# A hybrid decoder layer: the delta rule's triangular inverse and block merges for two heads at once, with a new order of issue

## The chip, the cores and the metric

One core of one Trainium2 chip. The metric is device microseconds of one execution, as the median of several runs.

## The reference

One layer works on 1024 tokens of width 1024 in 32-bit floats. After an RMS norm, one projection gives the columns of two groups of heads. Group A is a gated delta rule with 4 heads of width 128, group B a sparse attention with an indexer: each token scores all earlier tokens, keeps the best 256, and attends to them with 8 heads of width 64. Both outputs go through one output projection and a gated addition. What matters here is group A, in chunks of 64 tokens:

```
kkt = jnp.einsum('bhncd,bhnsd->bhncs', k_beta, k) * decay
a_mat = eye + jnp.where(strict, kkt, 0.0)
t_mat = lax.linalg.triangular_solve(a_mat, jnp.broadcast_to(eye, a_mat.shape),
                                    left_side=True, lower=True, unit_diagonal=True)
value = jnp.einsum('bhncs,bhnse->bhnce', t_mat, v_beta)
...
def step(state, inp):
    qd, kd, val, kcd, att, gl = inp
    v_new = val - jnp.einsum('bhcd,bhde->bhce', kcd, state)
    o = jnp.einsum('bhcd,bhde->bhce', qd, state) + jnp.einsum('bhcs,bhse->bhce', att, v_new)
    state = state * gl[..., None, None] + jnp.einsum('bhcd,bhce->bhde', kd, v_new)
    return state, o
```

`t_mat`, the inverse of a unit lower triangular matrix, is what the change computes in another grouping. The kernel uses chunks of 128 tokens, so 8 matrices of 128x128 per head; the result is the same.

## The kernel before, in words

The program is first recorded as a list of operations with what each depends on (`Plan`), and then issued in the order of a table of numbers, `TURNS` (line 76 and on): each number says which of the operations still left comes next. All engines' instructions are issued that way, in `issue`, so the trace shows line 556 for every one of them (554 after the change), and each engine's order is what the table says. Instructions are told apart by their tiles. PSUM tiles of one pool share a name in the trace: `s` for the small products of group A, `mm` for projections, `rec` for the recurrence's products, `po` for its outputs, `g` for the tail.

Stages in time: input norm, transposes and the gates' parameters; then the indexer's scores, to about 200 us; then a long middle of projections (`mm`, three matmuls for one full-precision product, from a high and a low half of both operands), beside which run group A's heads and the indexer's search for the 256th score; from about 560 us on the attention, the output projection and, as a tail, the gate.

In the middle, VectorE (`junk`) and ScalarE (`junka`) count how many scores lie above a threshold, pass after pass, until the threshold is found; after that VectorE makes a mask (`eq`, `cum`) and ScalarE copies it over the scores (`score<-eq`).

Each head h of group A goes through these steps:
- `gdn_s1` (line 1387): norms of q and k, decay matrices, the negated strict lower part `NB` of the 8 matrices (two tiles of four), the product `att`, the transposed and scaled values `v` (by ScalarE).
- `inverse` (line 1576), beside it: `NB` goes to DRAM and comes back as 16x16 diagonal blocks, one per partition group (`Bb`). Fifteen rounds of a product and a sum on VectorE (`ftmp<-Ub,Bb`, `Ub<-ftmp`) invert all blocks of the head. The result goes through DRAM to the tile `U32`, which holds 32x32 diagonal blocks.
- `merge` (line 1607) puts blocks of 16 together to 32, then 64, then 128. Each step is two products with a copy between: `w0` (64 instructions of 32x32x16, `s<-T,NB`), its copy `W0` by ScalarE (`W<-s` of 128x128), `x2` (`s<-U,W`), an addition and a transpose by VectorE (`U32`, `T32`); then `wa` (`s<-T,NB` of 32x32), two copies `W` by ScalarE (`W<-s` of 32x256), `wb` (`s<-W,U` and `s<-U,W`), copies into `T64` by VectorE and into `U` by ScalarE; then `wc` (64x64), its copy into `T64` by ScalarE (`T<-s` of 64x512), and `wd`, whose copy completes `U`.
- `gdn_s2` (line 1487): the recurrence over 8 chunks, a chain of three products (`rec`) a chunk with a VectorE step behind each (`r`, `vnew`, `S`).
- `gdn_out` (line 1551): the norm of the outputs and their way to DRAM.

In `merge` and `gdn_s2` the table puts projection matmuls between the products, so that TensorE has work while a copy is made. Before the change the four heads merge one after the other, at 262, 330, 408 and 486 us, and each head's recurrence runs in part beside the next head's merge.

In the tail, VectorE makes `m0Bl`, `h1Al` and `t1l` (low halves of operands of the last products), GpSimd makes other such halves (`low`, `sl`), and TensorE waits for them in the order of the table.

## Time and profile before

| what | value |
|---|---|
| median of 3 runs | 833.31 us (832.12 to 833.95) |
| the profiled execution, its own time | 835.29 us |
| its span in the trace | 833.3 us |
| mean granted clock of TensorE | 0.984 |
| busy share of PE, DVE, ACT, POOL | 97%, 80%, 71%, 65% |
| chain that ended last | PE 80%, DVE 9%, ACT 6%, issue 2% |
| half clock from, for | 75.62 us, 6.83; 410.13, 10.24; 741.22, 6.83; 829.96 to the end |
| waits of PE above 1.4 us in total | for `t1l` 3.4, for `g` 2.2, for `W` 2.2, for `ident` 1.5 |

The profiled execution took 835.29 us, 2.0 more than its span, and 2.0 more than the median of the runs. A trace row gives start, duration, engine, line, operation, output and inputs, shape, and in brackets the idle time before it and what ended that. Matmuls overlap with the one before them: one of 512 columns is shown with 0.39 to 0.40 us, but in a dense stretch the next starts 0.23 us later. The clock is recorded in windows of 3.41 us.

### The profile page before, as it was taken

To read this page: it belongs to the slowest core of one execution; us is meant where nothing else is said; L and a number is where in the kernel's file an instruction comes from. 1 tells how busy PE (TensorE), PEld (TensorE's weight loads), DVE (VectorE), ACT (ScalarE), POOL (GpSimd) and SP (SyncE) were. 2 spreads that over 40 slices of the span, in tenths; PEclk is the share of its full clock that TensorE was granted. 3 is DMA by queue.
4 is the path that set the end of the run, shared out by engine and by line. 5 is a ranking of instruction groups with operands and counts; after the bars stand their busy time and mean duration, and the time that the engine had idled before them with its cause. 6 is when DMAs were issued, how large, how long until landed. Compare 5 with 4: busy or idle time off the path is not lost.

```text
span 833.3 us, 14829 instructions
## 1 busy us (share of the span) xinstructions
PE 811.9 (97%) x5063; PEld 692.2 (83%) x5063; DVE 664.9 (80%) x1475; ACT 589.6 (71%) x1345; POOL 540.9 (65%) x704
## 2 busy tenths in 40 slices
PE   9998999999999999999999999999999999979996
PEld 6996999987888888888888888878888888768885
DVE  3698757888999999998768854699998786586676
ACT  5765466667999989999775543499886678765342
POOL 3487667524876677577748545368675647988982
PEclk9998999999999999999899999999999999989999
DMA  8963421001122233113312332676313421522453
GB/s 276 371 241 103 159 85 64 1 13 52 39 70 62 89 84 106 58 52 96 87 52 76 87 91 70 219 218 209 113 51 103 155 71 53 197 94 64 140 172 130
DMA packets 77868, 93.14 MB, mean 112 GB/s; under 512 B 24000, under 2 KB 40672, under 8 KB 77664
## 3 DMA queue, kind: packets, MB, share of 16 engines
q1 hardware_dynamic: 77792, 92.20, 34.4%
q8 instruction: 39, 0.64, 0.3%
q14 instruction: 37, 0.30, 0.1%
HBM read 66.72 MB, written 25.45 MB: 111 GB/s over the span
## 4 chain that ended last, share of the span: by engine, by line
PE 80%; DVE 9%; ACT 6%; issue 2%; DMA 1%; POOL 1%; SPq 0%; DVEq 0%; ACTq 0%
PE mm L556 44%; PE g L556 8%; PE lg L556 6%; PE s L556 5%; PE pv L556 4%; PE S L556 4%; PE pt L556 3%; PE c L556 3%; PE rec L556 2%; ACT junka L556 2%; PE po L556 2%; DVE c L556 1%; DVE xT L556 1%; DVE score L556 1%; DVE g L556 1%
## 5 line engine op out<-in xcount | busy, mean ns | idle before, releaser
L556 PE MATMUL mm<-hThi,hiw 128*128 128x512 f32 x400 | 156.8, 405 | 0.6 <-ACT fst L556 0.3
L556 PE MATMUL mm<-hTlo,hiw 128*128 128x512 f32 x400 | 156.3, 402 | 0.0
L556 PE MATMUL mm<-hThi,low 128*128 128x512 f32 x400 | 155.4, 401 | 0.0
L556 POOL TENSOR_TENSOR low<-raww,hiw 128x512 fp32r<-128x512 f32 (+1 forms) x93 | 123.7, 1335 | 43.0 <-ACT hiw L556 26.4
L556 ACT ACTIVATE junka<-score,nt 128x768 bf16<-128x768 int16 (+5 forms) x96 | 99.7, 1039 | 2.5 <-POOL scr L556 0.4
L556 PEld LDWEIGHTS mm<-hThi,hiw 128*128 128x128 f32 x400 | 75.8, 191 | 14.9 <-ACT fst L556 0.7
L556 PEld LDWEIGHTS mm<-hThi,low 128*128 128x128 f32 x400 | 75.9, 190 | 13.9
L556 PEld LDWEIGHTS mm<-hTlo,hiw 128*128 128x128 f32 x400 | 75.8, 190 | 13.6
L556 POOL TENSOR_SCALAR P<-P,rsum 128x128 f32<-128x128 f32 (+7 forms) x64 | 49.1, 773 | 38.0 <-DVE rsum L556 37.4
L556 DVE TENSOR_SCALAR_CACHE_REDUCE junk<-score,cand 128x384 bf16<-128x384 f32 (+2 forms) x96 | 71.1, 740 | 1.3
L556 ACT ACTIVATE hiw<-raww 128x512 fp32r<-128x512 f32 x91 | 56.7, 627 | 19.8 <-PE g L556 8.5
L556 POOL TENSOR_SCALAR nt<-acca,upa 128x1 f32<-128x1 f32 x96 | 36.8, 385 | 40.7 <-ACT junka L556 36.7
L556 ACT ACTIVATE relu<-lg 128x384 f32<-128x384 f32 (+1 forms) x80 | 41.1, 523 | 28.3 <-PE lg L556 24.6
L556 DVE SCALAR_TENSOR_TENSOR score<-relu,sm,score 128x384 f32<-128x384 f32 (+5 forms) x42 | 48.9, 1177 | 11.1 <-ACT relu L556 10.9
L556 ACT ACTIVATE P<-P,mn 128x128 f32<-128x128 f32 (+7 forms) x64 | 49.4, 773 | 11.8 <-DVE mn L556 11.4
L556 DVE TENSOR_TENSOR pl<-pt,ph 128x512 fp32r<-128x512 f32 x72 | 48.3, 685 | 8.2 <-ACT ph L556 6.7
L556 PE MATMUL S<-kst,qT 128*128 128x384 f32 (+2 forms) x192 | 52.3, 354 | 0.3 <-DVE mn L556 0.2
L556 ACT ACTIVATE ph<-pt 128x512 fp32r<-128x512 f32 x72 | 40.9, 594 | 10.4 <-PE pt L556 8.1
L556 ACT ACTIVATE fst<-mm 128x512 f32<-128x512 f32 (+2 forms) x61 | 29.9, 502 | 17.6 <-PE mm L556 17.3
L556 PE MATMUL pt<-ident,P 128*128 128x128 f32 x288 | 40.8, 274 | 0.3 <-POOL P L556 0.2
L556 PEld LDWEIGHTS S<-kst,qT 128*128 128x128 f32 x192 | 34.2, 189 | 7.0 <-DVE mn L556 1.5
L556 DVE SCALAR_TENSOR_TENSOR acc<-fst,cw,acc 128x512 f32<-128x512 f32 x48 | 38.7, 819 | 1.1 <-ACT fst L556 0.4
(434 smaller groups left out, 2507.3 us busy)
## 6 DMA issues: line engine op xcount, KB each, us to landing
raww<-in_w_ct_dram SPq DMA_DIRECT2D x50, 256.0 KB, 2.7
raww<-in_w_out_dram SPq DMA_DIRECT2D x32, 256.0 KB, 3.9
xt<-in_x_dram SPq DMA_DIRECT2D x8, 512.0 KB, 6.4
xc<-in_xc_dram SPq DMA_DIRECT2D x8, 512.0 KB, 7.1
pled<-plt SPq DMA_DIRECT2D x16, 256.0 KB, 4.7
rawi<-in_w_ct_dram SPq DMA_DIRECT2D x16, 256.0 KB, 2.9
pld<-pled SPq DMA_DIRECT2D x16, 256.0 KB, 2.6
out_dram<-gth SPq DMA_DIRECT2D x15, 256.0 KB
```

The costliest lines, as they stand in the source:

```text
L556: r = getattr(getattr(self.nc, o.eng), fn)(*[real(x) for x in args], **{k: real(v) for k, v in kw.items()})
```

## The change

Heads 0 and 1, and heads 2 and 3, now go through `inverse` and `merge` together. `inverse(hs)` has blocks of both heads in one `Bb` and one `Ub`, so that there are 30 products and 30 sums of twice the length instead of 60 and 60; the DMAs stay as many. `merge` takes `w0`, `x2`, `wa` and `wb` of both heads as one group into one PSUM tile, with one copy (W0: 128x256 instead of 128x128; W: two of 32x512 instead of two of 32x256) behind it; `wc` and `wd` stay one group per head. `U32`, `T32`, `W`, `W0` and `T64` are twice as long, and `NB` has four buffers instead of two. The new `gdn_group` runs `gdn_s1` of both heads up to the values, and then one merge for both. So the recurrence of a group's first head starts only behind the second head's preparation.

The table `TURNS` is new as a whole. Up to the end of the indexer's scores the instructions stand nearly where they stood; behind them the order is another one, in the tail also, where the computation is the same.

```diff
+GROUPS = ((0, 1), (2, 3))
...
-c-rlH2Yg(|dFRZ$UiR(2?Y%c(8-N8Ci{6RCf)1h*od5{1q7ftk0tDE=PKu<&B8t605~)H-BrRD<B-u(NpJhw&xy5oj=aNf)@z1t$J}16=U}Rg>Maf+fAOF9_+u5C&Z@&57
...
+c-rlH2XtK3x$fR)pWe^RIWuQ^AN5h08A+p2@4Z*ck|j6UisdFtw&mV!T)=<}#<&t}u)#E&M-LDPfi&9VLIQz=+z?2)cRh0RSSxw!9YM;?dT*t#b@LwnG^2ga(SP>-_y7O<
...
-            nb = NB[n] = half("NB", 2)
+            nb = NB[n] = half("NB", 4)
...
-        yield f"u{h}", UY
-        U = self.Uf[h % 2]
-        yield from self.merge(h, NB, self.U.pop(h), U)
-        self.s1[h] = dict(q=q, U=U, vt=vt, kh=kh, k=k, att=att, ssq=ssq, br=br)
+        self.pre[h] = dict(NB=NB, q=q, U=self.Uf[h % 2], vt=vt, kh=kh, k=k, att=att, ssq=ssq, br=br)
+
+    def gdn_group(self, hs):
+        for h in hs:
+            yield from self.gdn_s1(h)
+        yield f"u{hs[0]}", UY
+        d = [self.pre.pop(h) for h in hs]
+        yield from self.merge([x.pop("NB") for x in d], self.U.pop(hs[0]), [x["U"] for x in d])
+        self.s1.update(zip(hs, d))
...
-    def inverse(self, h):
-        nc, p = self.nc, self.gp
-        yield f"nb{h}"
-        NB = self.NB.pop(h)
+    def inverse(self, hs):
+        nc, p, n = self.nc, self.gp, len(hs)
+        for h in hs:
+            yield f"nb{h}"
         CH = 128 * 129
-        dN = self.tc.dram_tile([8 * CH], F32, name=f"dN{h}")
-        dU = self.dU[h % 2]
         mat = lambda d, n: d.raw(4 * n * CH, ap=[[128, 128], [CH, 4], [1, 128]])
         blk = lambda d, o, r: d.raw(o, ap=[[16 * 129, 64], [128, r], [1, 16]])
-        for n in range(2):
-            nc.sync.dma_start(mat(dN, n), NB[n])
-        Bb = p.tile([128, 16, 16], F32, name="Bb", bufs=1)
-        for g in range(2):
-            nc.sync.dma_start(Bb[64 * g:64 * g + 64], blk(dN, 0, 16))
-        nc.vector.memset(Bb.rearrange("p i l -> p (i l)")[:, 0:256:17], 1.0)
-        Ub = p.tile([128, 8, 16], F32, name="Ub", bufs=1)
-        tmp = p.tile([128, 8, 16], F32, name="ftmp", bufs=1)
-        nc.vector.tensor_copy(Ub, self.eyeb)
+        Bb = p.tile([128, 2, 16, 16], F32, name="Bb", bufs=1)[:, :n]
+        for i, h in enumerate(hs):
+            NB = self.NB.pop(h)
+            dN = self.tc.dram_tile([8 * CH], F32, name=f"dN{h}")
+            for e in range(2):
+                nc.sync.dma_start(mat(dN, e), NB[e])
+            for g in range(2):
+                nc.sync.dma_start(Bb[64 * g:64 * g + 64, i], blk(dN, 0, 16))
+        nc.vector.memset(Bb.rearrange("p h i l -> p h (i l)")[:, :, 0:256:17], 1.0)
+        Ub = p.tile([128, 2, 8, 16], F32, name="Ub", bufs=1)[:, :n]
+        tmp = p.tile([128, 2, 8, 16], F32, name="ftmp", bufs=1)[:, :n]
+        nc.vector.tensor_copy(Ub, self.eyeb[:, None].to_broadcast([128, n, 8, 16]))
         yield BY
         for l in range(1, 16):
-            nc.vector.tensor_tensor(tmp[:, :, :l + 1], Ub[:, :, :l + 1],
-                                    Bb[:, None, :l + 1, l].to_broadcast([128, 8, l + 1]), op=OP.mult)
-            nc.vector.tensor_reduce(Ub[:, :, l:l + 1], tmp[:, :, :l + 1], axis=AX.X, op=OP.add)
+            nc.vector.tensor_tensor(tmp[:, :, :, :l + 1], Ub[:, :, :, :l + 1],
+                                    Bb[:, :, None, :l + 1, l].to_broadcast([128, n, 8, l + 1]), op=OP.mult)
+            nc.vector.tensor_reduce(Ub[:, :, :, l:l + 1], tmp[:, :, :, :l + 1], axis=AX.X, op=OP.add)
             yield 1
-        for g in range(2):
-            nc.sync.dma_start(blk(dU, g * 8 * 128, 8), Ub[64 * g:64 * g + 64])
-        u = self.U[h] = p.tile([128, 8, 32], F32, name="U32", bufs=1)
-        for a in range(4):
-            nc.sync.dma_start(u[32 * a:32 * a + 32], dU.raw(a * 32 * 129, ap=[[128, 32], [CH, 8], [1, 32]]))
-        self.mark(f"u{h}")
-
...
+    def merge(self, NB, u, U):
+        nc, p, m = self.nc, self.gp, len(NB)
+        n = 8 * m
+        full = lambda nm: p.tile([128, 8 * 2, 32], F32, name=nm, bufs=1)[:, :n]
+        u = u[:, :n]
         quad = [slice(32 * a, 32 * a + 32) for a in range(4)]
         b32 = [(32 * a, 32 * a + 32, 32 * a + 64) for a in (0, 2)]
         flat = lambda t: t.rearrange("p a b -> p (a b)")
+        ps = lambda nm, w, n=n: self.ps_s(nm).rearrange("p a b -> p (a b)")[:, :n * w].rearrange("p (a b) -> p a b", b=w)
+        nb = lambda c, r, k: NB[c // 8][c // 4 % 2][r, c % 4, k]
+        T = full("T32")
         nc.vector.transpose(flat(T), flat(u))
         yield F1
         w0 = ps("w0", 16)
+        for c in range(n):
             for q in quad:
                 nc.tensor.matmul(w0[q, c], nb(c, q, q), T[q, c, 0:16], start=True, stop=True)
+        nc.scalar.activation(self.W0[:, :n, 0:16], w0, AF.Copy)
         yield F2
         x2 = ps("x2", 16)
+        for c in range(n):
             for q in quad:
                 nc.tensor.matmul(x2[q, c], self.W0[q, c], u[q, c, 16:32], start=True, stop=True)
         nc.vector.tensor_tensor(u[:, :, 16:32], u[:, :, 16:32], x2, op=OP.add)
+        T = full("T32")
         nc.vector.transpose(flat(T), flat(u))
         for a in (0, 1):
+            nc.gpsimd.tensor_copy(self.T64[quad[a], :n, 32 * a:32 * a + 32], T[quad[a]])
         yield F2
+        W = full("W")
         wa = ps("wa", 32)
+        for c in range(n):
             for i0, i1, i2 in b32:
                 nc.tensor.matmul(wa[i1:i2, c], nb(c, slice(i0, i1), slice(i1, i2)), T[i0:i1, c], start=True, stop=True)
         for i0, i1, i2 in b32:
             nc.scalar.activation(W[i1:i2], wa[i1:i2], AF.Copy)
+        for i in range(m):
+            for q in quad[::-1]:
+                nc.gpsimd.tensor_copy(U[i][q, :, q], u[q, 8 * i:8 * i + 8])
         yield F2
         wb = ps("wb", 32)
+        for c in range(n):
             nc.tensor.matmul(wb[32:64, c], u[32:64, c], W[32:64, c], start=True, stop=True)
             for i0, i1, i2 in b32:
                 nc.tensor.matmul(wb[i0:i1, c], W[i1:i2, c], u[i1:i2, c], start=True, stop=True)
+        nc.vector.tensor_copy(self.T64[32:64, :n, 0:32], wb[32:64])
+        for i in range(m):
+            for i0, i1, i2 in b32:
+                nc.scalar.activation(U[i][i0:i1, :, i1:i2], wb[i0:i1, 8 * i:8 * i + 8], AF.Copy)
         yield F2
         W2 = self.T64
+        wc = []
+        for i in range(m):
+            wc.append(ps("wc", 64, 8))
+            for c in range(8):
+                nc.tensor.matmul(wc[i][64:128, c], nb(8 * i + c, slice(0, 64), slice(64, 128)), self.T64[0:64, 8 * i + c],
+                                 start=True, stop=True)
+        for i in range(m):
+            nc.scalar.activation(W2[64:128, 8 * i:8 * i + 8], wc[i][64:128], AF.Copy)
         yield F2
+        wd = []
+        for i in range(m):
+            wd.append(ps("wd", 64, 8))
+            for c in range(8):
+                nc.tensor.matmul(wd[i][0:64, c], W2[64:128, 8 * i + c], U[i][64:128, c, 64:128], start=True, stop=True)
+        for i in range(m):
+            nc.scalar.activation(U[i][0:64, :, 64:128], wd[i][0:64], AF.Copy)
...
-            self.W0 = p.tile([128, 8, 32], F32, name="W0")
+            self.W0 = p.tile([128, 16, 32], F32, name="W0")
...
-            self.T64 = p.tile([128, 8, 64], F32, name="T64")
+            self.T64 = p.tile([128, 16, 64], F32, name="T64")
...
-            s1 = Chain(x for h in range(4) for x in self.gdn_s1(h))
-            si = Chain(x for h in range(4) for x in self.inverse(h))
+            s1 = Chain(x for hs in GROUPS for x in self.gdn_group(hs))
+            si = Chain(x for hs in GROUPS for x in self.inverse(hs))
```

Instructions: TensorE 4331 as before, VectorE 1306 (1378), ScalarE 1074 (1080), GpSimd 705 (709), SyncE 380 as before.

**TensorE, from wa to wb of the first merge.** Before, behind `wa` (the two rows of `s<-T,NB`) of the first head:

```order
L556 MATMUL s_2030<-T_0_1942,NB_1935 32x32 x8
L556 MATMUL s_2030<-T_0_1942,NB_1937 32x32 x8
L556 MATMUL mm_77<-hThi_124,hiw_107 128x512
L556 MATMUL mm_77<-hTlo_125,hiw_107 128x512
L556 MATMUL mm_75<-hTlo_125,hiw_113 128x512
L556 MATMUL mm_75<-hThi_124,low_114 128x512
L556 MATMUL mm_77<-hThi_124,low_108 128x512
L556 MATMUL s_2031<-W_1943,U_0_1941 32x32
L556 MATMUL s_2031<-U_0_1941,W_1943 32x32 x2
```

After, from the filler behind `x2` of the first group:

```order
L554 MATMUL mm_76<-hThi_124,hiw_111 128x512
L554 MATMUL mm_75<-hTlo_125,hiw_111 128x512
L554 MATMUL mm_75<-hThi_124,low_112 128x512
L554 MATMUL mm_75<-hThi_124,hiw_113 128x512
L554 MATMUL mm_76<-hTlo_125,hiw_111 128x512
L554 MATMUL mm_76<-hThi_124,low_112 128x512
L554 MATMUL s_2038<-T_0_1939,NB_1930 32x32 x8
L554 MATMUL s_2038<-T_0_1939,NB_1932 32x32 x8
L554 MATMUL s_2038<-T_0_1939,NB_1934 32x32 x8
L554 MATMUL s_2038<-T_0_1939,NB_1935 32x32 x8
L554 MATMUL s_2039<-W_1940,U_0_1938 32x32
L554 MATMUL s_2039<-U_0_1938,W_1940 32x32 x2
```

Five projection matmuls stood between `wa` and `wb`; now `wb` follows `wa` directly, and six stand between `x2` and `wa`.

**ScalarE, from W to the copy of wc in the first merge.** Before, in the first head (`T_0<-s` of 64x512 is the copy of `wc`, which `wd` reads):

```order
L556 ACTIVATE W_1943<-s_2030 32x256 x2
L556 ACTIVATE junka_1975,acca_1976<-score_120,nt_0_1977 128x768
L556 ACTIVATE hiw_109<-raww_116 128x512
L556 ACTIVATE scr_1934<-scr_1930,gg_98 128x128 x2
L556 ACTIVATE U_1948<-s_2031 32x8x32 x2
L556 ACTIVATE scr_1933<-scr_1929,gg_98 128x128
L556 ACTIVATE fst_129<-accq_1990 128x512
L556 ACTIVATE scr_1933<-scr_1929,gg_98 128x128
L556 ACTIVATE T_0_1928<-s_2032 64x512
```

After, in the first group, up to the same copy:

```order
L554 ACTIVATE junka_1972,acca_1973<-score_120,nt_0_1966 128x1024
L554 ACTIVATE scr_1929<-scr_1925,gg_98 128x128
L554 ACTIVATE junka_1972,acca_1973<-score_120,nt_0_1974 128x768
L554 ACTIVATE junka_1972,acca_1973<-score_120,nt_0_1974 128x896
L554 ACTIVATE junka_1972,acca_1973<-score_120,nt_0_1974 128x1024
L554 ACTIVATE U_1945<-s_2039 32x8x32
L554 ACTIVATE junka_1972,acca_1973<-score_120,nt_0_1966 128x768
L554 ACTIVATE U_1990<-s_2039 32x8x32
L554 ACTIVATE U_1945<-s_2039 32x8x32
L554 ACTIVATE junka_1972,acca_1973<-score_120,nt_0_1966 128x896
L554 ACTIVATE U_1990<-s_2039 32x8x32
L554 ACTIVATE T_0_1923<-s_2037 64x512
```

Instead of one pass of the count (`junka`) there are six in the stretch from the copies `W` to the copy of `wc`, and two copies `U` became four.

**ScalarE, around W0 of the third head.** Before (`W_0<-s` is the copy of `w0`):

```order
L556 ACTIVATE junka_1975,acca_1976<-score_120,nt_0_1969 128x896
L556 ACTIVATE v_1960<-s_2030,irk_1953 128x128 x2
L556 ACTIVATE scr_1934<-scr_1930,gg_98 128x128
L556 ACTIVATE score_120<-eq_1980 128x384
L556 ACTIVATE W_0_1927<-s_2032 128x8x16
L556 ACTIVATE junka_1975,acca_1976<-score_120,nt_0_1969 128x1024
```

After, around the copy of the second group's `w0`:

```order
L554 ACTIVATE score_120<-eq_1977 128x384
L554 ACTIVATE fst_130<-mm_75 128x512
L554 ACTIVATE v_2002<-s_2039,irk_1995 128x128 x3
L554 ACTIVATE fst_129<-mm_76 128x512
L554 ACTIVATE v_2003<-s_2037,irk_1995 128x128
L554 ACTIVATE W_0_1922<-s_2038 128x16x16
L554 ACTIVATE v_2003<-s_2037,irk_1995 128x128 x2
L554 ACTIVATE score_120<-eq_1977 128x384
```

The mask copy `score<-eq` stood directly ahead of W0; now it stands behind, and the one before it is separated from W0 by six other copies.

**TensorE, in the recurrence of the third head.** Before, the sixth of its eight chunks:

```order
L556 MATMUL rec_2036<-S_2010,acc_0_1936 128x128
L556 MATMUL mm_75<-hThi_124,hiw_107 128x512
L556 MATMUL mm_75<-hTlo_125,hiw_107 128x512
L556 MATMUL mm_75<-hThi_124,low_108 128x512
L556 MATMUL mm_75<-hThi_124,hiw_107 128x512
L556 MATMUL rec_2036<-r_2011,U_1948 128x128
L556 MATMUL s_2031<-T_0_1928,NB_1935 64x64 x4
L556 MATMUL s_2031<-T_0_1928,NB_1937 64x64 x4
L556 MATMUL rec_2036<-vnew_2012,kh_1952 128x128
L556 MATMUL mm_77<-sel_86,fst_131 128x2 x4
L556 MATMUL rec_2036<-S_2013,acc_0_1936 128x128
```

After, the same chunk:

```order
L554 MATMUL rec_2043<-S_2017,acc_0_1931 128x128
L554 MATMUL mm_77<-sel_86,fst_131 128x2 x3
L554 MATMUL rec_2043<-r_2018,U_1945 128x128
L554 MATMUL mm_75<-hThi_124,hiw_107 128x512
L554 MATMUL mm_75<-hTlo_125,hiw_107 128x512
L554 MATMUL rec_2043<-vnew_2019,kh_1949 128x128
L554 MATMUL po_2044<-S_2017,accq_1946 128x128
L554 MATMUL mm_75<-hThi_124,low_108 128x512
L554 MATMUL s_2037<-ident_81,o_2023 128x128 x2
L554 MATMUL rec_2043<-S_2020,acc_0_1931 128x128
```

The chain is `rec<-S`, `rec<-r`, `rec<-vnew` and the next `rec<-S`. Before, four projection matmuls, eight products of `wc` and four small products (`mm<-sel,fst`) filled its three steps; now three small products, two projection matmuls, and one projection matmul with three products of 128 columns fill them.

179 lines of the change are left out of this document (80 added, 99 removed).

## The prediction

> **What bounds the kernel now.** I read the page's busy times first, then its clock row, then the waits of TensorE, then the stretches around the places where the clock is low, and last the instructions there.
>
> ```profile
> span 833.3 us, 14829 instructions
> PE 811.9 (97%) x5063; PEld 692.2 (83%) x5063; DVE 664.9 (80%) x1475; ACT 589.6 (71%) x1345; POOL 540.9 (65%) x704
> PEclk9998999999999999999899999999999999989999
> ```
>
> TensorE is busy for 97% of the span and no other engine for more than 80%. So only two things can move the time: intervals in which TensorE stands, and intervals in which it runs at a lower clock. The clock row has three dents: the fourth, the 20th and the 36th slice. The second lies near 410 us, inside the part that is changed. The waits of TensorE, with total, times and longest:
>
> ```profile
> PE g L556 <- DVE t1l L556: 3.4, 1, 3.4
> PE s L556 <- ACT W L556: 2.2, 3, 1.4
> ```
>
> The second row belongs to the merges (x2 waits for the copy of w0). The windows around the clock's dents, with busy time of PE, PEld, DVE, ACT, POOL, then the clock:
>
> ```profile
> core 0: us, PE busy (x) PEld busy (x) DVE busy (x) ACT busy (x) POOL busy (x), PEclk, DMA share, GB/s
> 72.20:75.61 3.41, 1.87 (x9) 1.31 (x9) 3.38 (x5) 0.00 (x0) 2.71 (x4) 1.00 0.00 0
> 406.71:410.12 3.41, 2.34 (x76) 1.84 (x74) 2.72 (x4) 1.58 (x6) 3.33 (x4) 1.00 0.74 231
> 410.12:420.36 10.24, 9.93 (x119) 8.44 (x120) 5.01 (x8) 7.83 (x20) 6.79 (x13) 0.50 0.24 79
> 485.22:488.63 3.41, 3.02 (x138) 2.50 (x137) 2.17 (x6) 1.75 (x6) 0.06 (x1) 1.00 0.57 202
> 730.98:734.39 3.41, 2.37 (x11) 1.65 (x10) 2.46 (x3) 2.73 (x6) 3.41 (x4) 1.00 0.26 82
> 737.80:741.21 3.41, 0.89 (x4) 0.39 (x3) 3.35 (x6) 1.71 (x3) 0.67 (x1) 1.00 0.71 235
> 741.22:748.04 6.82, 5.95 (x14) 4.69 (x15) 6.16 (x9) 4.65 (x9) 6.66 (x6) 0.50 0.20 74
> 260.00:280.00 20.00, 19.41 (x315) 15.82 (x313) 18.89 (x50) 18.99 (x57) 12.09 (x23) 1.00 0.20 68
> ```
>
> The half clock followed windows of 3.41 us in which TensorE was busy for 1.87, 2.34 and 0.89 us, and did not follow 2.37 and 3.02. So a window that holds about 1.07 us of idle time costs half a clock for 6.8 or 10.2 us. [...] The window at 406.71 is the third head's merge:
>
> ```profile
> 408.15 1.51 DVE L556 SCALAR_TENSOR_TENSOR eq<-score,cand,eq 128x384 bf16<-128x384 f32 x1
> 408.32 0.73 PE L556 MATMUL s<-T,NB 32*32 32x16 f32 x64
> 409.69 0.52 ACT L556 ACTIVATE score<-eq 128x384 f32<-128x384 bf16 x1 [1.83 <-DVE eq L556]
> 410.12 0.26 ACT L556 ACTIVATE W<-s 128x128 f32<-128x128 f32 x1
> 410.43 1.05 PE L556 MATMUL s<-U,W 32*32 32x16 f32 x64 [1.38 <-ACT W L556]
> ```
>
> w0 ran at 408.32. Its copy W0 stood on ScalarE behind a mask copy, which waited for a comparison on VectorE. TensorE stood 1.38 us until x2 at 410.43, and the clock fell.
>
> **The change, part by part**, against the profiled execution's own 835.29 us (span 833.3 and about 2.0 around it; 2.0 above the median of 833.31, to which I carry the difference over).
>
> *Half clock.* 10.24 us at half rate cost 10.24 x 0.5 = 5.1 us. In the new order W0 of the second group has no mask copy directly ahead of it, and x2 follows w0 directly with a wait of about 0.5 us (next item), like the fourth head's merge in window 485.22, which kept its clock. So **-5.1**; if the cover fails, the whole comes back.
>
> *Waits for W0.* The three waits above sum to 2.2 us. Rows of a copy and of the waits beside it:
>
> ```profile
> 487.44 0.73 PE L556 MATMUL s<-U,W 32*32 32x16 f32 x64 [0.39 <-ACT W L556]
> L556 ACT ACTIVATE W<-s 32x256 f32<-32x256 f32 x8 | 3.0, 376 | 0.9 <-PE s L556 0.8
> 267.94 0.78 ACT L556 ACTIVATE W<-s 32x256 f32<-32x256 f32 x2 [0.34 <-PE s L556]
> L556 ACT ACTIVATE T<-s 64x512 f32<-64x512 f32 x4 | 2.4, 592 | 1.2 <-PE s L556 1.2
> ```
>
> A wait of 0.39 is the copy's 0.26 (row 410.12 above) and 0.13 of hand-over. The new W0 copy has 256 columns; the 32x256 row gives 0.38, with hand-over 0.5, twice: 1.0 for 2.2: **-1.2**.
>
> *Half as many groups of small products.* w0, x2, wa and wb of four heads were 16 groups and become 8. What a group costs beyond its products:
>
> ```profile
> 329.24 0.40 PE L556 MATMUL mm<-hTlo,hiw 128*128 128x512 f32 x1
> 329.57 0.73 PE L556 MATMUL s<-T,NB 32*32 32x16 f32 x64
> 330.23 0.50 PE L556 MATMUL mm<-hThi,low 128*128 128x512 f32 x1
> 330.56 0.40 PE L556 MATMUL mm<-hThi,hiw 128*128 128x512 f32 x1
> 330.80 0.39 PE L556 MATMUL mm<-hTlo,hiw 128*128 128x512 f32 x1
> ```
>
> Projection matmuls start every 0.23 to 0.24 us; into the group the step is 0.33, and out of it the next step is 0.33 again: 0.2 us a group, 8 x 0.2 = 1.6. Where groups now stand side by side a part of it is inside the waits, so I take **-1.4** (ends 0 and -1.6).
>
> *wb waits for W in the first group.* Before, five projection matmuls (5 x 0.23 = 1.2 us) stood between wa and wb of the first head. Now nothing does, and W is two copies of 32x512 instead of 32x256. A pair of 376 ns copies took 0.78 in all (row 267.94), since they overlap; by the 512-column row (592 ns) I put a pair of the new ones at 1.1 as an estimate, and with hand-over 1.2: **+1.2** (ends 0.8 and 1.4). In the second group eight matmuls (1.8 us) cover it.
>
> *wd waits for the copy of wc in the first group.* Behind the W copies, ScalarE has six passes of the top-k count ahead of the copy T64 that wd reads:
>
> ```profile
> L556 ACT ACTIVATE junka<-score,nt 128x1024 bf16<-128x1024 int16 x16 | 18.4, 1149 | 0.6 <-DVE score L556 0.2
> L556 ACT ACTIVATE junka<-score,nt 128x896 bf16<-128x896 int16 x16 | 16.6, 1039 | 0.2
> L556 ACT ACTIVATE junka<-score,nt 128x768 bf16<-128x768 int16 x16 | 14.9, 933 | 0.8 <-POOL scr L556 0.4
> L556 ACT ACTIVATE U<-s 32x256 f32<-32x256 f32 x8 | 3.0, 369 | 0.9 <-DVE T L556 0.8
> 271.16 1.14 PE L556 MATMUL s<-T,NB 64*64 64x64 f32 x16
> ```
>
> From the end of wa: the W pair 1.1, passes 2 x (1.15 + 1.04 + 0.93) = 6.2, four U copies 1.5, T64 0.6: 9.4 us, and ScalarE has no slack there (18.99 of 20 us busy in the row for 260 to 280). TensorE has between wa and wd 22 projection matmuls (5.1), wc (1.1, row 271.16), wb about as much, and the wait of 1.2: 8.5 less what overlaps, some 8.2. The difference is **+1.2** (ends 0, if ScalarE was ahead, and 2.0).
>
> *U32 and T32.* The add of x2 (0.29 for 128 columns) and the transpose double their columns. Six matmuls (1.4 us) stand between x2 and wa of the first group; I estimate the two VectorE steps at 0.5 and 0.8 with their hand-overs beside that, so I take **+0.3**, with 0 and 0.6 as ends. The 30 + 30 long steps of the inverse save VectorE some 10 us of busy time, off the chain: nothing.
>
> *The recurrence of the third head* now starts behind the second merge and is pressed together, since it must end where it ended before. The step from one of its products to the next, over VectorE:
>
> ```profile
> 505.94 0.38 PE L556 MATMUL rec<-vnew,kh 128*128 128x128 f32 x2
> 506.86 0.40 PE L556 MATMUL rec<-S,acc 128*128 128x128 f32 x2
> 507.80 0.40 PE L556 MATMUL rec<-r,U 128*128 128x128 f32 x2
> ```
>
> These two steps took 0.92 and 0.94 us, with the second waited for. In the new order seven of the 23 steps hold only about 0.67 us of TensorE's work and one 0.55. 7 x 0.26 + 0.38 = 2.2, some of it taken up by earlier slack: **+2.0** (ends 1.0 and 2.5).
>
> *All other turns* (DMAs, fillers, the indexer's masks, the tail) change place without any row that says which way: **0**, with 3 to either side.
>
> Sum: -5.1 - 1.2 - 1.4 + 1.2 + 1.2 + 0.3 + 2.0 = **-3.0 us**: 832.3 on the profile, **830.3** as a median.
>
> **Rivals.** (B) *The half clock moves to the first group.* A window that holds the wait of 1.2 us for W whole has TensorE busy for 2.2 us, under the 2.34 that was followed by half a clock; it lies whole in one window in (3.41 - 1.2)/3.41 = 65% of the placements, if it is that long. The wait at wd (1.2) can do the same. For it: the third head's merge did just this. Against: TensorE was busy for only 2.37 us in the window at 730.98 and kept its clock, so the margin is thin and the size of the wait decides. Price 6.83 x 0.5 = 3.4 to 5.1 us, less the 1.2 at wd, which a slower TensorE doesn't wait for: -3.0 + 2.2 to 3.9, so 832.5 to 834.2, no change within what can be told.
>
> (C) *The tail gains as well.* The longest wait of all (3.4 us, for t1l) and the last costly half clock stand in the tail:
>
> ```profile
> 733.20 4.79 DVE L556 SCALAR_TENSOR_TENSOR m0Bl<-x,g,m0Bh 128x512 fp32r<-128x512 f32 x1
> 736.12 1.32 POOL L556 TENSOR_TENSOR low<-rawg,hiw 128x512 fp32r<-128x512 f32 x1
> 741.96 1.64 DVE L556 SCALAR_TENSOR_TENSOR m0Bl<-x,g,m0Bh 128x512 fp32r<-128x512 f32 x1
> ```
>
> One m0Bl took 4.79 us and ended (737.99) only when GpSimd's back-to-back chain had ended (737.44). Its result isn't what TensorE waits for, but t1l stands behind it; TensorE then stood 3.4 us, was busy for 0.89 of 3.41, and ran at half rate for 6.83. If the new turns break that meeting, 3.4 + 3.4 = 6.8 us more go: 823.5. Nothing in the order removes GpSimd's chain, so this is the less likely. [...]
>
> (D) *The other side: the tail loses.* In the new order all four m0Bl stand ahead of the t1l for the third of the group's outputs, where two did, and two of them side by side. If a second one meets GpSimd's chain, VectorE loses another 4.79 - 1.5 = 3.3 us and TensorE waits for it, with another window or two at half rate (3.4): -3.0 + 6.7 = +3.7, so 837.0. It decides from two stretched ones on; with one, as now, it costs nothing new.
>
> (E) *The half clock of 410 us has another cause and stays.* Then -5.1 falls away: +2.1, 835.4, slower. For it: in a window with 2.37 us busy the clock held, and 2.34 is hardly less. Against it: every drop in the rows above follows the emptiest stretch in its neighbourhood. [...]
>
> **How the numbers follow.** A measurement of this kernel tells a change from about 0.2%, or 1.7 us: 831.6 to 835.0 is no change. Forecast 0.42, B 0.26, C 0.10, D 0.17, E 0.05. The unknown turns (3 either side) spread each case. Faster: two thirds of the forecast (0.28), C 0.10, a quarter of B (0.06): 0.44. Same: the rest of the forecast but a little (0.12), most of B (0.16), a little of D and E (0.03): 0.31. Slower: D and E mainly (0.19), some of B and of the forecast (0.06): 0.25. The range leaves out most of C below and the worse half of D above: 825.5 to 836.5.
>
> **What would show it.** In the new profile: no clock of 0.5 near 420 to 450 us; one wait of x2 for W0 of about 0.5 us in each group; one wait of wb for W of 1.2 us and one of wd for T64 of about 1.2 in the first group; waits of rec for r, vnew or S of 2 us in all in the third head. The forecast is wrong if the clock row has a dent near 320 us (B), if the t1l wait is gone (C) or doubled (D), or if the third head's dent is still there (E); and wrong in its terms if the merges' waits are those but the sum of waits elsewhere moved by more than 3 us.

## The result, and the profile after

The changed kernel took **844.01 us** (median of 4 runs, 843.22 to 844.28) against 833.23 for the kernel before (4 runs): ratio 1.0129, 95% interval 1.0111 to 1.0147. It is slower by 10.8 us, above the range of the prediction (825.5 to 836.5). The profiled execution took 844.28 us.

The page of the changed kernel, with its span, its busy times, its clock row and the row of the queue q8, which it names instruction (transfers, MB, share):

```profile
span 842.6 us, 14733 instructions
PE 812.1 (96%) x5063; PEld 685.1 (81%) x5063; DVE 659.4 (78%) x1403; ACT 587.5 (70%) x1339; POOL 550.9 (65%) x700
PEclk9999999999999995999999899999999999999999
q8 instruction: 39, 0.64, 0.3%
```

TensorE is busy for 812.1 us, as before (811.9). So the whole loss is standing time: 842.6 - 812.1 = 30.5 us, where it was 833.3 - 811.9 = 21.4, 9.1 more of the span's 9.3. (The 4331 that the section on the change gives for TensorE is not the page's number: the page counts 5063 matmuls for both kernels, and the sums below go by it.) The clock row has its dents in other places: the 16th slice (the first group) is at 0.5, the 23rd (the second) at 0.8, and those at 75, 410 and 741 us are gone. The waits of TensorE, total, times, longest:

```profile
PE s L554 <- issue: 6.3, 2, 3.9
PE s L554 <- DVE kh L554: 2.3, 1, 2.3
PE s L554 <- ACT W L554: 2.3, 3, 1.3
PE s L554 <- DVE att L554: 2.0, 1, 2.0
```

The first row is the news: TensorE stood 6.3 us in two places while nothing that the profile records was missing. `kh` and `att` are new too, 4.3 us together. The 3.4 us for `t1l` are gone, and the 2.2 for `g` at the start also. All waits that the two lists name come to 23.1 us after and 14.7 before, so they hold 8.5 of the 9.1 us; what is not in these rows are many waits of at most 1.3 us each. The timeline of TensorE at the two merges (the bracket is the standing time before the row):

```profile
310.57 1.26 PE L554 MATMUL s<-T,NB 32*32 32x16 f32 x128 [0.44 <-DVE T L554]
312.33 0.58 PE L554 MATMUL s<-U,W 32*32 32x16 f32 x47 [0.49 <-ACT W L554]
316.76 1.30 PE L554 MATMUL s<-U,W 32*32 32x16 f32 x81 [3.86 <-issue]
...
324.06 0.26 PE L554 MATMUL s<-W,U 32*32 32x32 f32 x1 [1.29 <-ACT W L554]
...
475.19 0.93 PE L554 MATMUL s<-U,W 32*32 32x16 f32 x89 [0.49 <-ACT W L554]
478.60 0.73 PE L554 MATMUL s<-U,W 32*32 32x16 f32 x39 [2.48 <-issue]
```

`x2` is one group of 128 products over one operand pair, and it breaks in the middle: after 47 products in the first group, after 89 in the second. Windows of TensorE around both places, busy time of all its matmuls, then the clock:

```profile
core 0: us, PE busy (x), PEclk, DMA share, GB/s
309.40:312.82 3.42, 2.48 (x179) 1.00 0.90 227
312.82:333.30 20.48, 15.33 (x285) 0.50 0.08 26
466.42:469.83 3.41, 1.58 (x9) 1.00 0.32 47
473.25:476.66 3.41, 2.27 (x218) 1.00 0.58 209
476.66:483.49 6.83, 4.89 (x50) 0.50 0.27 92
```

And of the matmuls into the small `s` tiles alone, in the two windows ahead of the drops:

```profile
309.40:312.82 3.42, 1.75 (x175) 1.00 0.90 227
473.25:476.66 3.41, 2.19 (x217) 1.00 0.58 209
```

The clock fell behind windows that were busy for 2.48 and 2.27 us, and stayed up behind one busy for only 1.58. What tells these three apart is what they were busy with: of 2.48, 1.75 were the tiny products. In all, 15.33 + 4.89 = 20.2 us of busy time ran at half the clock. Projection matmuls start every 0.42 to 0.43 us there (from 318.59 to 320.29) and every 0.22 to 0.23 us ahead of the merge (from 309.29 to 309.74), so I estimate its worth at half, 10.1 us. Before, it was 9.93 + 5.95 from the prediction's rows and, from the start,

```profile
75.62:82.45 6.83, 5.67 (x17) 0.50 0.00 1
```

5.67, so 21.55 us, worth 10.8. By this sum the half clock costs as much as before. It only changed places.

**Where the instructions were.** q8 made 39 transfers of together 0.64 MB, 16.4 KB each. The profile doesn't say whose instructions they are. I take them for pieces of TensorE's program, since they come in step with it: 5063 matmuls and as many weight loads are (5063 + 5063) / 39 = 260 instructions a piece, or 130 products with their loads, and from the first transfer (25.43 us, behind 103 matmuls) to the last (808.39, behind 4932) there are 127 matmuls to each. And the stops stand whole pieces apart. All matmuls up to the stop in the first group (the count is in the brackets):

```profile
0.00:316.70 316.70, 303.90 (x1754) 0.99 0.35 116
```

The second group's stop stands behind product 3031 of the program. In the experiments below, the trace shows 28 stops of this kind in 11 kernels. All stand at whole multiples of 128 products from product 1754, within 5 products; 128 products with their loads are 256 instructions, and the trace records 43 to 45 other instructions of TensorE, which I take for the difference.

The DMA view of the changed kernel for the 3.9 us up to 314.4, and then for the one microsecond behind it (queue, packets, MB, share of the engines):

```profile
q1 hardware_dynamic: 506, 0.91, 83.9%
...
q8 instruction: 1, 0.02, 5.9%
q1 hardware_dynamic: 7, 0.01, 2.3%
```

Up to 314.4 the DMA engines were 83.9% busy with data (the last of `U32`'s small loads, then 256 KB each for `zad`, `raww` twice, `scr` and `z`), and q8 moved nothing. When the data were through, one piece came (at 314.43, in 0.95 us), and 1.4 us behind it `x2` went on at 316.76. The two stops together cost 6.3 us.

### The profile page after: what moved, and what is told of

It reads as the page before. It is cut to its first block, busy times and chain, and to the rows that moved or that the text cites. A ratio compares the mean times of both kernels' runs of the same rounds, so it can differ in the third digit from the quotient of the medians.

```text
span 842.6 us, 14733 instructions
## 1 busy us (share of the span) xinstructions
PE 812.1 (96%) x5063; PEld 685.1 (81%) x5063; DVE 659.4 (78%) x1403; ACT 587.5 (70%) x1339; POOL 550.9 (65%) x700
## 4 chain that ended last, share of the span: by engine, by line
PE 68%; DVE 16%; DMA 5%; ACT 4%; issue 3%; SPq 2%; POOL 1%; DVEq 0%; ACTq 0%; POOLq 0%
PE mm L554 34%; PE g L554 7%; PE lg L554 5%; PE s L554 4%; PE pv L554 4%; PE S L554 3%; PE pt L554 3%; PE rec L554 3%; PE c L554 3%; SPq L554 2%; DVE junk L554 2%; DVE ftmp L554 2%; DMA xt<-in_x_dram 2%; PE po L554 2%; DVE c L554 1%
## 5 line engine op out<-in xcount | busy, mean ns | idle before, releaser
L554 POOL TENSOR_TENSOR low<-raww,hiw 128x512 fp32r<-128x512 f32 (+1 forms) x93 | 126.3, 1360 | 74.9 <-ACT hiw L554 51.9
L554 PE MATMUL mm<-hThi,hiw 128*128 128x512 f32 x400 | 159.8, 409 | 1.1 <-DVE fst L554 1.1
L554 POOL TENSOR_SCALAR P<-P,rsum 128x128 f32<-128x128 f32 (+7 forms) x64 | 49.2, 776 | 30.9 <-DVE rsum L554 30.5
L554 POOL TENSOR_SCALAR nt<-acca,upa 128x1 f32<-128x1 f32 x96 | 43.5, 457 | 33.5 <-ACT junka L554 31.0
L554 ACT ACTIVATE relu<-lg 128x384 f32<-128x384 f32 (+2 forms) x80 | 40.8, 524 | 25.0 <-PE lg L554 21.3
L554 ACT ACTIVATE P<-P,mn 128x768 f32<-128x768 f32 (+7 forms) x64 | 49.4, 773 | 4.0 <-DVE mn L554 3.8
```

What stands on the lines that cost most here:

```text
L554: r = getattr(getattr(self.nc, o.eng), fn)(*[real(x) for x in args], **{k: real(v) for k, v in kw.items()})
```

## The experiments

In this section, and in the expectations quoted in it, A and B are the theories of the experiments, not the cases B to E of the prediction. The theory from these rows, **A** (instruction supply): w0 and x2 of two heads are 256 products, with their loads two pieces of program, consumed at 1.26 us for 128; TensorE runs out of instructions, and the next piece waits behind data (A1) or is late of itself (A2). The rivals of this theory: **B**, the stop belongs to the operands, the copy W0 or `U32`; and that the loss comes from other new turns (`kh`, `att`). Every median below has the kernel before measured on the same chip, at 829.7 to 833.7 us.

### The products of the kernel before, issued twice

```diff
-        for c in range(8):
+        for c in [*range(8)] * 2:
```

This in w0 and in x2 of the kernel before: the same values go a second time into the same place, and the result is the same.

> The kernel before, with each product of w0 and x2 issued twice over (the same products into the same places, so the result is unchanged): 128 rows of w0 and 128 of x2 per head, as in the grouped kernel, but with the order, the tiles and the DMAs of before. Theory A (TensorE runs out of instructions: about 150 small products empty what has been loaded, and the next load takes several us): a stop of 1 to 4 us that the waits call issue appears inside x2 of at least two of the four heads, where x2 stands directly behind w0 (first, third and fourth head), with a half clock behind a long one; the run is 5 to 20 us longer, beyond the 4 x 0.9 = 4 us that the added products take. Theory B (the stop belongs to the grouped tiles or to their DMAs): no stop inside x2, and about 4 us longer.

It took 850.63 us, 17 more than the kernel before on that chip (833.74). The wait row, and the first merge, where the kernel before has no stop:

```profile
PE s L556 <- issue: 5.9, 5, 1.9
```

```profile
260.19 1.26 PE L556 MATMUL s<-T,NB 32*32 32x16 f32 x128
261.84 0.51 PE L556 MATMUL s<-U,W 32*32 32x16 f32 x39 [0.39 <-ACT W L556]
263.98 0.93 PE L556 MATMUL s<-U,W 32*32 32x16 f32 x89 [1.63 <-issue]
```

The operands were the old ones and a head's copy had the old size; only the number of instructions had grown, and the stops came in all four heads: in x2 behind products 1498, 2265, 3031 and 3669 of the program, and one of 0.15 us in wa behind 3797. Counted from the start of w0 that is after 128 + 39 = 167, 235, 241 and 147 products, so it isn't a fixed number of them that runs out, but, as I read it, the piece that ends there. So this B falls, and A stands. Some 4 of the 17 us are the added products' own time, by the expectation.

### One and a half times

```diff
-        for c in range(8):
+        for c in [*range(8), *range(4)]:
```

> The kernel before, with half of the w0 and x2 products issued a second time (the same values into the same place): 96 + 96 products a head, between the 64 + 64 of the kernel before, without a stop, and the 128 + 128 of the run with all twice, with five stops, longest 1.9 us. Supply theory: the stops came after 167 to 175 products, so 192 still run out: one to four stops, shorter than 1.9 us. If the stop hangs on the length of one group (over 64 products) and not on the sum, it is as with 128. If there is none, the limit lies between 192 and 256.

847.16 us (one run; 829.73 for the kernel before on that chip).

```profile
PE s L556 <- issue: 3.4, 3, 1.7
```

```profile
266.97 0.38 PE L556 MATMUL s<-U,W 32*32 32x16 f32 x25 [1.70 <-issue]
```

The first merge broke after 96 + 71 products, which is product 1498 again: the same piece end as in the run before, since the program ahead of this w0 is the same. So 167 is no limit by itself. With 64 + 64 a head (before) no such end brings a stop; with 96 + 96 three do, with 128 + 128 five. The time rose by 17.4 us, with all of them twice by 16.9, though the stops are fewer (3.4 us against 5.9) and the stretches of half clock behind the merges shorter, together 23.9 us against 37.5. These rows don't explain that; each time is a single run, and runs of the kernel before went from 825.1 to 836.0 us on this chip and from 826.5 to 835.4 on the other.

### Other matmuls between w0 and x2

In the first group 19 projection matmuls were put between w0 and x2, 11 in the second, and what follows was moved down:

```diff
 MATMUL s_2039<-T_0_1939,NB_1935 32x16 x16
-MATMUL s_2037<-U_0_1938,W_0_1922 32x16 x64
 MATMUL mm_76<-hThi_124,hiw_111 128x512
...
+MATMUL mm_75<-hTlo_125,hiw_113 128x512
+MATMUL s_2037<-U_0_1938,W_0_1922 32x16 x64
```

> The changed kernel with the same operations and another order: 19 projection matmuls instead of none between w0 and x2 of the first group and 11 (and two transposes) in the second, and the rest of each merge and the recurrence behind it moved down by as much. Theory A (instructions run out): the stops inside x2 (3.86 and 2.48 us) go or fall below 0.5 us, with the half clock of 20.5 us in the first group and of 6.8 us in the second: 844.0 less 6.3, less about 10, plus up to 4 for a tighter recurrence: 829 to 835. Theory B (x2 waits for data, for instance the second head's U32): the stop inside x2 goes as well if the data come later by time alone, so only its size tells; theory C (the loss is spread over the new order, and the stop is a symptom): 840 or more.

A miss: 856.58 us, ratio 1.0296 (1.0231 to 1.0361). The stops shrank to 1.5 and 0.3 us (under 0.5 was expected), but the rows that had been moved down met new waits:

```profile
PE s L551 <- DVE T L551: 2.8, 2, 2.1
...
PE mm L551 <- ACT fst L551: 1.8, 1, 1.8
PE s L551 <- issue: 1.8, 2, 1.5
PE rec L551 <- DVE S L551: 1.7, 2, 1.2
```

I read these rows so that one row of TensorE can't be moved by 4 us here without the other engines' rows.

### Data transfers later in SyncE's order

```diff
 DMA raww_116<-in_w_ct_dram 128x512
-DMA raww_115<-in_w_ct_dram 128x512
 DMA scr_1925<-gcd 128x512
+DMA raww_115<-in_w_ct_dram 128x512
```

Three such transfers of the first group and five of the second were put later in the table of turns. In SyncE's own row that changes little, the swap above in the first group and a few more in the second.

> The changed kernel with five DMAs of the first group's place (one weight load, scr and z) and of the second's (two weight loads, one store and two z) issued behind x2 instead of ahead of it; engines' orders as they were. Theory A1 (the load of instructions waits behind the data that the DMA engines move): the stops inside x2 shrink from 3.86 and 2.48 us to 1.5 or less, the half clock with them, and the run falls to 832 to 839. Theory A2 (the load takes about 6 us from request to use whatever else is moved): stops stay within 0.5 us of what they were and the time within 2 us of 844.

842.09 us (1.0122, 1.0066 to 1.0179), the `issue` wait 5.8, longest 4.1. This looked like A2, but it told nothing apart: the transfers didn't start later. SyncE issued the first group's, from `zad` to `z`, at 308.24 to 310.56 us in the changed kernel and at 307.45 to 309.82 here. It goes through its own row as its waits let it, so a later turn in the table is not a later start. To hold the data back, a wait was needed. (No row shows when a piece is asked for, so A2's 6 us from request to use are an estimate; from the start of w0 to x2's going on it was 6.2 us in the changed kernel, 310.57 to 316.76.)

### Data transfers held until x2 is done

```diff
+HOLD = {2910: 2942, 4707: 4457}
...
+                if o.i in HOLD:
+                    self.tc.add_manual_dep(r.ins, self.ops[HOLD[o.i]].ins[-1].name, mybir.DependencyInfo(
+                        mybir.DependencyClass.Sync, mybir.DependencyReason.DATA), reason="hold")
```

The first transfer behind `U32`'s loads waits for the last product of x2, and with it those queued behind it.

> The changed kernel, with the data transfers that follow the eight small loads of U32 in each group made to wait for the last product of x2 (5 transfers a group, data unchanged). Theory A1 (TensorE's next 16 KB of instructions wait behind a burst of data transfers on the same DMA engines): the transfer that started at 314.43 now starts near 311, the stop inside x2 shrinks from 3.9 us to 1 us or less, the one in the second group from 2.5 to 0.5 or less, the half clock of 20.5 us there to 7 or less, and the time falls to 834 to 840. Theory A2 (the instructions come late of themselves, whatever else the DMA engines do): the stop stays at 3.5 to 4.1 us and the time within 2 us of 844. Against both: if a held transfer is needed sooner than it can come, TensorE waits for it at a new place, and the time rises.

842.03 us (1.0091, 1.0058 to 1.0123). The DMA view of this run between 311.3 and 312.4 us, and TensorE's row behind its stop:

```profile
q8 instruction: 1, 0.02, 5.3%
```

```profile
313.58 0.92 PE L552 MATMUL s<-U,W 32*32 32x16 f32 x81 [1.13 <-issue]
```

Nothing else moved in that stretch: the piece came 3.1 us earlier (0.5 of that is w0's own earlier start), where A1 had put it, and the stop fell from 3.86 to 1.13, in the second group from 2.48 to 1.36:

```profile
474.88 0.72 PE L552 MATMUL s<-U,W 32*32 32x16 f32 x39 [1.36 <-issue]
```

So the data are the cause of 3.8 of the 6.3 us, which is A1. But 2.5 us remained with the data held, at the first stop with nothing but the piece moving, where A1 had left room for 1.5: that part I put down to A2, the piece late of itself. The half clock behind the first merge was 3.41 and 10.24 us, not the 7 expected, and the time missed the 834 to 840. It fell by 2 to 3 us (2.0 between the medians, 3.2 by the ratios), and the intervals of this run and of the changed kernel (1.0111 to 1.0147) overlap. What I see against it: the held data were now missed elsewhere. ScalarE stood 4.81 us for `raww`, and W, which is queued behind that pass, came later, so that TensorE's wait for W rose to 2.2.

### TensorE's rows respaced, VectorE's two steps earlier, all three together

Three other matmuls between w0 and x2, six ahead of wa, six between wa and wb:

```diff
-MATMUL s_2037<-U_0_1938,W_0_1922 32x16 x64
...
 MATMUL mm_75<-hThi_124,low_112 128x512
+MATMUL s_2037<-U_0_1938,W_0_1922 32x16 x64
```

> The changed kernel, with TensorE's rows alone respaced: in the first group three other matmuls between w0 and x2, about six more ahead of wa, six between wa and wb, five ahead of wc, and wc of the second stage ahead of wd; in the second group four between w0 and x2. Cover theory: the wait of wb for W (1.29) and those of x2 for W (0.49 each) go, about 2 us; supply theory: three matmuls give the instruction transfer only 0.7 us more, so the stop shrinks from 3.9 to about 3 and the half clock near 313 stays. Both together: 839 to 842. Rival: as in the run with 19 matmuls moved, the later rows pay for it with new waits (T, fst, r): 844 to 850.

843.83 us (1.0115, 1.0080 to 1.0150): the first stop stayed (3.7; the second fell to 1.5), the waits for W went, and one of 3.4 us for T came in their place. The `kh` and `att` steps, by four rows each:

```diff
+TENSOR_TENSOR kh_1994<-s_2039,ekd_102 128x512
 TENSOR_SCALAR junk_1964,acc_1965<-score_120,cand_0_1969 128x384
...
-TENSOR_TENSOR kh_1994<-s_2039,ekd_102 128x512
```

> The changed kernel, with two VectorE steps taken earlier in its order: kh ahead of about four rows in the stage before the first group, att ahead of about four in the second. If the two longest waits for VectorE (2.3 us for kh at 270, 2.0 us for att at 466) come from the places alone, they go and the time falls by 3 to 4.5 us, to 839.5 to 841. If VectorE is late as a whole there, the waits only move to the steps that now stand behind: 843 to 846.

842.09 us (1.0093, 1.0058 to 1.0129). The two waits went, and these came:

```profile
PE s L551 <- DVE acc L551: 1.4, 1, 1.4
PE s L551 <- DVE accq L551: 1.3, 1, 1.3
```

The time lies between the two ranges expected, but the waits moved to other steps: VectorE is late as a whole ahead of each merge. All three together:

> The changed kernel with all three: the held transfers, the respaced rows of TensorE and the two earlier VectorE steps. If the three causes are separate and add up: the stop under 1 us, no half clock over 7 us near 313, no wait for kh or att over 1 us, 828 to 835, at or under the kernel before. If the instruction supply isn't mended by the hold: 838 to 843.

841.29 us (1.0097, 1.0063 to 1.0131): the stops were down to 1.5 and 0.6, but TensorE waited 3.6 us for W and 1.9 for T. The gains don't add up.

### The gaps filled, twice

First with the data held until w0 only, eight matmuls between w0 and x2, and ScalarE's order changed:

> The changed kernel, with the data transfers behind U32's loads held until the last product of w0 (not of x2), eight other matmuls of 0.23 us between w0 and x2 in the first group and six with two transposes in the second, six ahead of wa, five between wa and wb, and ScalarE's copies of wa (W) ahead of the pass over hiw that waits for held data. Supply theory: from the request to the first use the instructions take about 3.3 us on idle DMA engines, and TensorE now has 1.3 (w0) + 1.9 + 0.5 (the 47 products that it still has) = 3.7 us of work in that time, so the stop inside x2 is under 0.3 us; with W's wait under 0.5 us the half clock near 313 is at most 3.4 us; group 0 costs 6 to 9 us of lag instead of 16, the time is 834 to 838. If the half clock comes without any stop or wait over 0.5 us, the stops aren't its cause, and the time stays at 840 or more. If ScalarE's new order makes its passes late, a wait for the top-k threshold or hiw shows up behind the merge.

A miss: 845.32 us. The 3.3 us from request to first use are an estimate; in the run with the data held until x2 is done, x2 went on 3.5 us behind the start of w0 (310.11 to 313.58). The new order was not what I had meant (it put the copy W behind six passes of the top-k count instead of ahead of them), and x2 stood 4.8 us for a step of ScalarE behind the held data. In the next one the other matmuls were taken ahead, so that nothing of the merge moves past a step that it needs, and W, U and T64 stand ahead of the passes:

```diff
 ACTIVATE W_1940<-s_2038 32x512 x2
 ACTIVATE junka_1972,acca_1973<-score_120,nt_0_1966 128x1024
+ACTIVATE hiw_109<-raww_116 128x512
...
-ACTIVATE junka_1972,acca_1973<-score_120,nt_0_1974 128x768
```

> The changed kernel, with the data transfers behind U32's loads held until the last product of w0, and in the first group eight matmuls of 0.23 us moved ahead between w0 and x2, six ahead of wa, five between wa and wb, five between wb and wc, wc of the second head ahead of wd, and ScalarE's copies of W, of wb and of wc ahead of the pass over the held data and of the top-k passes; in the second group eight rows between w0 and x2. Supply theory: x2 runs in one piece (no stop over 0.5 us in either group). If stops and waits are what halves the clock, then with no wait over 1 us between 309 and 325 it is halved for at most 3.4 us there, and the first group costs 5 to 9 us of TensorE's lag instead of 16: 834 to 838. If the clock is halved for 10 us or more with no such wait, something else halves it: 841 or more. A wait of wd for T64 or of a later row for a top-k threshold would show that ScalarE's passes are the next bound.

841.41 us (1.0124, 1.0074 to 1.0174), again above the 834 to 838. Its merge, and its windows:

```profile
314.80 0.93 PE L552 MATMUL s<-U,W 32*32 32x16 f32 x89 [0.24 <-issue]
320.45 0.69 PE L552 MATMUL s<-T,NB 32*32 32x32 f32 x31 [2.47 <-issue]
```

```profile
318.89:322.30 3.41, 1.85 (x36) 1.00 0.08 25
322.30:342.78 20.48, 19.47 (x178) 0.50 0.12 40
```

The stop in x2 shrank from 3.86 to 0.24, and the clock, which had fallen at 312.82, held through w0 and x2. But now the held data came out at 313 to 318 us, in front of the next piece of instructions, and the same stop stood one piece later, in wa: behind product 1882, which is 1754 + 128. The half clock followed it there. So a long stop in the merge and the half clock go together in both places.

### No data in front of any piece

As the last one, with one `raww` loaded ahead of `U32`'s round trip, and the first group's other data held until the last product of wb:

```diff
 DMA dU_64<-Ub_1937 64x8x16
+DMA raww_116<-in_w_ct_dram 128x512
...
 DMA zad<-fst_130 128x512
-DMA raww_116<-in_w_ct_dram 128x512
```

> As the run with the filled gaps, but one of the data transfers is loaded ahead of U32's round trip and the others are held until the last product of wb, so that no data stands in front of any of the merge's instruction transfers in the first group (there the stop had moved from x2 into wa: 2.5 us, behind the transfers that were held only until w0); ScalarE's pass over hiw and two over scr stand behind its copies of the merge. If the stops alone halve the clock: no stop over 0.5 us up to wb, no half clock between 309 and 325 (at most 3.4 us), the first group's lag under 8 us instead of 16, and 833 to 838. If the clock is halved for 10 us or more without a stop or wait over 1 us in the 7 us before it, the stops are not its cause. If the data now come too late, a wait on hiw, low, scr or a top-k threshold shows behind wb.

841.42 us (1.0134, 1.0097 to 1.0172), not the 833 to 838 expected. TensorE at w0, at the breaks of x2 and wa, and at the first long wait behind the merge; then its windows:

```profile
313.10 1.26 PE L552 MATMUL s<-T,NB 32*32 32x16 f32 x128 [2.43 <-DVE T L552]
...
317.22 0.93 PE L552 MATMUL s<-U,W 32*32 32x16 f32 x89 [0.37 <-issue]
320.95 0.69 PE L552 MATMUL s<-T,NB 32*32 32x32 f32 x31 [0.56 <-issue]
...
337.95 0.80 PE L552 MATMUL mm<-sel,fst 128*128 128x2 f32 x3 [5.58 <-ACT fst L552]
```

```profile
312.20:315.61 3.41, 2.51 (x134) 1.00 0.02 5
332.69:336.10 3.41, 0.00 (x0) 1.00 0.00 0
336.10:342.92 6.82, 4.97 (x20) 0.50 0.35 115
```

Both stops, and a third in wb behind product 2010, are down to about half a microsecond, and between 309 and 332 us the clock doesn't fall. Two other things were then late. `U32`'s round trip came out later behind the `raww` that was put ahead of it (VectorE stood 3.32 us for its loads, 1.33 in the changed kernel), so w0 waited 2.43 us for T instead of 0.44. And ScalarE: `fst` stands behind five passes of the top-k count that had to make way for the merge's copies, and TensorE stood 5.58 us for it, which cost the clock again. The mean granted clock of this run is 0.993, above the 0.984 of the kernel before, so here the loss is standing time alone. So the price of the first group was paid in instructions, in data or in ScalarE's passes, and each time it came to about the same: the four runs with held data (842.03, 841.29, 841.41, 841.42 us) can't be told apart, and the fifth, with ScalarE's order mistaken, is 845.32.

### The ends of the kernel before in the new order

No operation changes; the rows behind 670 us of TensorE's work (and, in the second run, also those ahead of 100) take the new turns. For instance, VectorE in the tail:

```diff
+SCALAR_TENSOR_TENSOR m0Bl_5906<-x_0_5916,g_0_5911,m0Bh_5905 128x512
+TENSOR_TENSOR g_7419<-x_0_7406,g_7419 128x512
 TENSOR_TENSOR g_7421<-x_0_7406,g_7421 128x512
...
-SCALAR_TENSOR_TENSOR m0Bl_5906<-x_0_5916,g_0_5911,m0Bh_5905 128x512
-TENSOR_TENSOR t1l_7399<-g_7421,t1h_7398 128x512
```

> The kernel before, with only the turns behind 670 us of TensorE's work taken from the changed kernel. Turns theory: the tail's share alone, 828 to 830, the wait for t1l gone, the half clock at 75 us still there. Rival as for the run with both ends: 831 to 835.

> The kernel before, with its merges and everything between 100 and 670 us of TensorE's work as they were, but the turns of all operations ahead of 100 us and behind 670 us taken from the changed kernel (no operation added or removed). Turns theory: the ends gain by the order alone what TensorE's lag shows, about 3 us at the start (no waits for g, gg and sh, no half clock at 75 us) and 4 to 5 in the tail (no wait of 3.4 us for t1l, no half clock at 741): 825 to 828, faster than both kernels. Rival: the gain at the ends belongs to the data that the merges leave behind, or to where the clock's windows happen to lie: 831 to 835.

The tail alone: 830.09 us, ratio 0.9959 (0.9939 to 0.9979). Both ends: **828.74 us**, 0.9950 (0.9931 to 0.9969), the fastest kernel of the study, though 0.7 us above the range expected. The clock rows of the two, in this order:

```profile
PEclk9998999999999999999989999999999999999999
```

```profile
PEclk9999999999999999999889999999999999999999
```

The wait for `t1l` is gone in both, the start's dent in the second. The tail's dent is gone in the first; in the second, 3.41 us of half clock are left of its 6.83, too short to show in the row:

```profile
733.12:736.53 3.41, 3.26 (x8) 0.50 0.50 159
```

So the new turns at the ends are worth about 0.5%, 4.2 us by the ratio; the two intervals overlap, so what the start alone adds isn't shown. The second run has the new ends around the old merges, so the changed kernel differs from it only in the joint `inverse` and `merge` and in the turns between 100 and 670 us. These cost the 10.8 us that were measured and these 4.2: some 15 us.

## Why the prediction was wrong

**The step that failed** is the first of the sum: "x2 follows w0 directly with a wait of about 0.5 us (next item), like the fourth head's merge in window 485.22, which kept its clock." That window holds one head's 64 + 64 products. The new group has 128 + 128, and both things that hang on the count changed: TensorE, by theory A, ran out of instructions (6.3 us, for which the sum has no term; by the run with held data 3.8 of them are the data's doing), and the two windows ahead of the drops held mostly tiny products (1.75 of 2.48 us and 2.19 of 2.27). The third head's dent did go, as forecast. What came for it was rival B in place, but not in mechanism or price: I had it hang on the 1.2 us for W and put it at 3.4 to 5.1 us; it came with the stop, in both groups, and cost 10.1, with the 6.3 of standing beside it.

**My reading of the clock was wrong too.** I took 2.34 us busy in 3.41 as the point at which it falls. In the changed kernel it held behind 1.58 and fell behind 2.48. Worked out over all 15 traces, window by window: if 8 ns of busy time are taken off for each product of w0, x2, wa and wb (the value that fits best; 128 of them in w0 are busy for 1.26 us, 9.8 ns each), then of 48 windows at full clock with less than 1.4 us left all 48 were followed by half the clock, of 31 with 1.4 to 1.9 us 11 were, and of 3464 with more, 1. With nothing taken off, 12 with more than 1.9 us were. So by this fit the tiny products count for next to nothing; it is a fit to the traces, and no run was made for it alone. It would also explain why the window from 309.40 in the changed kernel was followed by the drop when its only gaps were 0.44 and 0.49 us.

**The other terms.**
- W0 waits: 0.49 and 0.49, forecast 0.5 each. Right.
- wb waits for W: 1.29, forecast 1.2. Right, and as forecast only in the first group. One reading behind it was not: two copies of 376 ns that take 0.78 us don't overlap (2 x 376 is 752), and the new pair took 1.19 us, not 1.1.
- wd waits for T64: none, forecast 1.2. I take it that TensorE was late itself, by the stop and the half clock. In the last of the experiments, where it wasn't, ScalarE's passes were what it waited for.
- U32 and T32: no wait of wa, forecast 0.3.
- The third head's recurrence: none of the 2.0. The window over it is full:

```profile
494.00:516.00 22.00, 22.00 (x144) 1.00 0.11 37
```

- Half as many groups: not measured by itself.
- All other turns, 0 with 3 to either side: the ends gained 4.2, and VectorE's lateness ahead of the merges cost 2.3 + 2.0. So the sum was near nothing, but of two parts larger than the bound.

**Rival C** (the tail gains) came true, in another way than the one I priced. VectorE's stretched step is still there, but no `t1l` is late behind it:

```profile
737.34 4.55 DVE L554 SCALAR_TENSOR_TENSOR m0Bl<-x,g,m0Bh 128x512 fp32r<-128x512 f32 x1
745.05 0.69 DVE L554 TENSOR_TENSOR t1l<-g,t1h 128x512 fp32r<-128x512 f32 x1 [1.18 <-ACT t1h L554]
```

I had said that nothing in the order removes GpSimd's chain, and that was so: GpSimd is busy from 728.78 to 744.41 us with no gap over 0.1 us. What changed is that no `t1l` is late. Why the step takes 4.55 us isn't shown: C and D took the chain for the cause, but beside it two other steps of 128x512 took 0.68 and 0.73 us (at 742.54 and 743.13). The run with the tail alone puts the gain at 3.4 us, not 6.8. D fell: no wait for `t1l` is left. E fell too: the half clock near 410 us is gone with the new merges, and it stands in both runs that have the new turns around the old ones (from 413.25 and from 408.86 us).

What stays open: which change would win back the 10.8 us, since each run that shortened the stop lost most of the gain to new waits; why the clock stayed down for 20.5 us behind the first group's stop, in the run with the gaps filled even with TensorE busy for 19.47 of them, when it came back after 6.8 behind other stops; and, if single runs can be trusted that far, why one and a half times the products cost as much as twice.

## What to carry to other kernels

Before you join groups of tiny matmuls, count their instructions, not only their waits: here two groups of 128 products, each 1.26 us long, came to what is, by the count, the end of a piece of program before the next piece was there, and in the first merge that piece came at 314.4 us behind data, at 311.3 with those data held. When a wait has no releaser in the profile, look at the instruction queue and at what the DMA engines were doing. And test a new order of issue apart from the new computation: here the order's ends were worth 0.5%, and they hid more than a quarter of what the joint merge and the turns around it cost.
